# A hybrid attention layer on one core: the order's model learns VectorE's holds and TensorE's short waits, and two more pairs of heads add their halves on 128 rows

## The chip, the cores and the metric

The kernel runs on one core of a Trainium2 chip. The metric is the device time of one execution in microseconds. The engines are named as in the profile: PE is TensorE's matrix multiplication and PEld its weight loads, DVE is VectorE, ACT is ScalarE, POOL is GpSimd, SP is SyncE, which here issues transfers.

## The reference

One layer for 512 tokens of width 1024. A normalised input is multiplied by one wide matrix; its columns feed two token mixers and two gates. Branch a is latent attention with 8 heads (a low-rank query and key/value, a shared rotary key), branch b is 8 heads over the 128 keys that a small indexer picks for each query, with a bias by relative position. Both are causal by chunks of 64.

```python
h = rmsnorm(x, norm_g[l])
(q_lat, c_kv, k_rope, z_a, q_b, k_b, v_b, z_b, q_idx, k_idx, w_idx, gate_a, gate_b) = \
    jnp.split(h @ w_in[l], cuts, axis=-1)
...
y_a = mla_attention(q_nope, q_pe, k_nope, k_pe, v_a, pos) * jax.nn.silu(z_a)
y_b = dsa_attention(q_b, k_b, v_b, q_idx, k_idx, w_idx, rel_bias, pos, topk) * jax.nn.silu(z_b)
merged = (jax.nn.sigmoid(gate_a) * (y_a @ w_o_a[l])
          + jax.nn.sigmoid(gate_b) * (y_b @ w_o_b[l]))
x = x + merged @ w_out[l]
return rmsnorm(x, final_g)
```

## The kernel before, in words

Every operand of a product is split into a rounded high part (a cast on ACT, L382) and a low part, the rest (a subtraction on DVE or POOL, `lo_part`, L417 and L419). A product is three matmuls: high by high, high by low, low by high (`mm3`, L497). Many of the projections go in pairs, and the final product in blocks, by seven half-size products in place of eight (`seven`, `output`), whose sums DVE and POOL form.

The order of the work is not written out by hand. Each part of the kernel is a generator that yields steps, and a planner, `Flow`, runs them all at once while the program is made. It keeps a model of the time: for each engine when it is free, for each buffer when it was written and read last and by whom. For each waiting step it works out the earliest start, `start`, and takes the step with the least key: that start, plus 0.01 us for each unit of the thread's priority, and small handicaps for POOL and for changing the engine that holds the port that DVE and POOL share (`shares`). The instructions then stand on each engine in that order, and the engines wait for each other by semaphores. So a change to the model's numbers changes the order on all engines, and nothing in what is computed.

The steps that the change touches:

- `tt`, `stt` and `ts` make VectorE's two-input, three-input and one-input steps. `few` adds 0.12 us to a step on fewer than 128 rows.
- `with_values` multiplies the probabilities of one head by its values. The product of head h stands in a bank of PSUM on 64 rows of its own and 64 of its partner (the two halves are the high and the low part of the values). ACT copies the partner's rows to its own rows of a buffer `s_tmp`, and DVE adds 64 rows from the bank and 64 from the buffer into `s_y`. For pairs of heads in `YBOTH` both halves are copied by ACT, and when both heads of the pair are done one step adds 128 rows from SBUF, on DVE or POOL. Before, these are pairs 0, 1 and 2 of branch b.
- `rest` in `seven` makes the last four of the seven products, with priority `PREST`.
- `multiplier` works through a queue of projections, `jobs`, with priority 12. Behind the entries of `QUEUE` come the 16 projections of the branches' outputs (`branch_out`); the jobs that load and split `w_out` are put behind those numbered in `OUT_AT`, and the rest come last. `fetcher` issues the loads of the same queue on SP, as far as there are buffers (`NRAW`, `ROCAP`).
- `SPARE`, `TCAP` and `PCAP` set how many buffers a class of steps must leave free or may hold.

The phases in time: the first loads and the input's latents (to 46 us), projections beside the indexer's scores and branch a's heads (to some 180 us), the values of branch b (to 217), branch b's heads beside projections in pairs (to 331), the branches' output projections (to 377), the final product and norm.

Of the kernel before, what the change touches and what calls it, by code (L numbers as in the profile page):

```python
# [78 lines left out]
class View:  # L79
# [11 lines left out]
        return View(self.buf, self.ap.rearrange(pattern, **kw))  # L91

    @property
    def n(self):
        n = 1
        for s in self.ap.shape[1:]:
            n *= s
        return n


class Step:
# [5 lines left out]
    pair = False  # L107
    pbias = None
    rush = 0.0

    def __init__(self, options, outs, ins):
        self.options, self.outs, self.ins = options, outs, ins


class Get:
# [39 lines left out]
class Flow:  # L155
# [9 lines left out]
    def __init__(self, order):  # L165
        self.free = {"PE": 0.6, "ACT": 0.73, "DVE": 0.93, "POOL": 0.73, "SP": 0.73}
        self.hw, self.dma = 0.73, 0.0
        self.pbias = PEARLY
        self.port, self.holder, self.paired, self.pair = 0.0, None, 0.0, None
        self.order = order  # L170
        self.threads = []

    def spawn(self, gen, prio):
        t = Thread(gen, prio)
# [12 lines left out]
    def start(self, step, eng):  # L187
        s = 0.0
        for b in step.ins:
            if not b.written and b not in step.outs:  # L190
                return math.inf
            s = max(s, b.w + (RAW_LAG.get(eng, 0.0) if b.by == eng else self.lat(b.by, eng)))
            if b.bank and eng != "PE":
                for e, r in b.reads.items():
                    if e != eng:
                        s = max(s, r + self.lat(e, eng))
        for b in step.outs:
            if not eng == b.by == "SP":
                s = max(s, b.w + self.lat(b.by, eng))
            for e, r in b.reads.items():  # L200
                s = max(s, r + self.lat(e, eng))
        self.due = max(self.free[eng], s + SETTLE.get(eng, 0.0))
        s = max(s, self.free[eng])
        if self.shares(step, eng):
            s = max(s, self.port)
            if FENCE and eng == "POOL":
                if s < self.paired + FENCE:
                    s = max(s, self.paired + 0.17)
        return s

    @staticmethod
    def shares(step, eng):
# [2 lines left out]
    def run(self, stop=None):  # L215
        while self.threads:
            if stop and stop():
                return
            moved = False
            for t in sorted(self.threads, key=lambda t: t.prio):  # L220
                if isinstance(t.req, Get):
                    b = t.req.pool.give(t.req)
                    if b is not None:
                        self.advance(t, b)
                        moved = True
                elif isinstance(t.req, Until) and t.req.cond():
                    self.advance(t, None)
                    moved = True
            if moved:
                continue  # L230
            best = None
            for t in self.threads:
                if isinstance(t.req, Step):
                    for i, (eng, dur, emit) in enumerate(t.req.options):
                        s = self.start(t.req, eng)
                        change = SWITCH * (self.shares(t.req, eng) and eng != self.holder and s < self.port + 0.01)
                        key = (max(s, self.due) + change + BIAS * t.prio + t.off + YIELD * self.shares(t.req, eng) * (eng == "POOL") - t.req.rush, t.prio)
                        if len(t.req.options) > 1:
                            fin = s + dur + {"POOL": self.pbias if t.req.pbias is None else t.req.pbias, "ACT": t.req.abias}.get(eng, 0.0)
                            cand = (fin, s, eng, dur, emit, key)  # L240
                        else:
                            cand = (0.0, s, eng, dur, emit, key)
                        if i == 0 or cand[0] < mine[0]:
                            mine = cand
                    if best is None or mine[5] < best[1][5]:
                        best = (t, mine)
            if best is None or best[1][1] == math.inf:
                raise RuntimeError("stuck: " + "; ".join(f"{t.gen.__name__}@{t.gen.gi_frame.f_lineno} {type(t.req).__name__} {getattr(t.req, 'cls', '')}" for t in self.threads))
            t, (_, s, eng, dur, emit, _) = best
            step = t.req  # L250
            step.made = emit()
            step.fenced = s < self.paired + FENCE
            if eng == "SP":

                self.free["SP"] = s + 0.05
                kind = 0 if step.ins and step.outs else 1 if step.outs else 2
                if s > 25.0:
                    at = max(self.hw, s)
                    self.hw = at + 0.59
                    self.dma = max(self.dma, at + 1.0) + dur * SLOWER[kind]  # L260
                    end = self.dma + LAND[kind] + step.late
                else:
                    self.hw = max(self.hw, s) + (0.475 if kind else 0.65)
                    self.dma = max(self.dma, self.hw + 0.65) + dur
                    end = self.dma + (1.5 if s < 0.77 or dur < 0.05 else 2.15 if s < 10.0 else 1.8 if s < 20.0 else 1.0) + step.late
            else:
                self.free[eng] = end = s + dur
                if self.shares(step, eng):
                    self.port, self.holder = end, eng
                    if eng == "DVE":  # L270
                        self.paired, self.pair = end, step.made
                    elif step.fenced and self.pair:
                        self.order(step.made, self.pair)
                if step.moves:
                    self.dma = max(self.dma, end + (1.0 if eng == "POOL" else 0.8)) + step.moves
                    end = self.dma + (1.5 if s < 0.77 or step.moves < 0.05 else 2.0 if s < 3.0 else 1.0) + step.late
            for b in step.ins:
                b.r = b.reads[eng] = max(b.r, end)
                if isinstance(b, Part):
                    b.whole.r = b.whole.reads[eng] = max(b.whole.r, end)  # L280
            for b in step.outs:
                b.w = max(b.w, end)
                b.written, b.by = True, eng
                if isinstance(b, Part):
                    b.whole.w, b.whole.written, b.whole.by = max(b.whole.w, end), True, eng
            self.advance(t, None)
# [3 lines left out]
PEARLY = -0.5  # L290
BIAS = 0.01
SETTLE = {}
YIELD = 0.15
SWITCH = 0.1
JITTER = 0
SEED = 1
DRAWN = random.Random(SEED)
TC_ARGS = {}

# [2 lines left out]
def tile_block(ctx: ExitStack, tc: tile.TileContext, a: dict, out: bass.AP, bias_dram: bass.AP):  # L302
# [70 lines left out]
    def few(x):  # L373
        return 0.12 if x.ap.shape[0] < P else 0
# [38 lines left out]
    def tt(dst, x, y, op, engs=("DVE",)):  # L413
        opts = []
        for e in engs:
            if e == "DVE":
                opts.append(("DVE", 0.07 + 0.00104 * x.n + few(x), lambda: nc.vector.tensor_tensor(dst.ap, x.ap, y.ap, op=op)))  # L417
            else:
                opts.append(("POOL", 0.15 + 0.0021 * x.n, lambda: nc.gpsimd.tensor_tensor(dst.ap, x.ap, y.ap, op=op)))  # L419
        step = Step(opts, bufs(dst), bufs(x, y))  # L420
        step.pair = not (in_ps(x) or in_ps(y))
        return step

# [3 lines left out]
    def stt(dst, x, s, y, op0, op1):  # L427
        step = Step([("DVE", (0.13 if isinstance(s, View) else 0.07) + 0.00104 * x.n,
                      lambda: nc.vector.scalar_tensor_tensor(dst.ap, x.ap, sc(s), y.ap, op0=op0, op1=op1))],  # L429
                    bufs(dst), bufs(x, s, y))  # L430
        step.pair = not (in_ps(x) or in_ps(y))
        return step

    def ts(dst, x, s1, s2, op0, op1=None):
        t = 0.1 + (0.00104 if in_ps(x) else 0.00052) * x.n + few(x) + 0.03 * isinstance(s1, View)
        kw = {} if op1 is None else {"op1": op1}
        step = Step([("DVE", t, lambda: nc.vector.tensor_scalar(dst.ap, x.ap, sc(s1), s2, op0, **kw))],
                    bufs(dst), bufs(x, s1))
        step.pair = not in_ps(x) and x.n > 8
        return step  # L440

# [2059 lines left out]
QPOOL = 1  # L2501
PHCAP = 7
WCAP = 10
TCAP = 5
PTOPK = 17.0
PSCORE = 8.0
PFILL = 12.0
PHEAD = 8.0
OUT_AT = (0, 1, 2, 4, 6, 8, 10)
ORDER = [0,1,2,3]  # L2510
QUEUE = 'ga0 ga1 pe ma0 ga2 za0 va1 va0 ma1 ga3 za1 ma2 ga4 ga5 ma3 za2 za3 sb0 VB GA6 GA7 SB1 GB0 GB1 SB2 ZB0 ZB1 GB2 GB3 SB3 GB4 GB5 ZB2 ZB3 gb6 ou ou gb7 ou'
LATE = 0.75
# [2 lines left out]
ADDW = ()  # L2515
ADDP = ()
ADDV = ()
RUSH = 0.2
YBOTH = ((), (0, 1, 2))
BADD = 0  # L2520
AHEAD = 0
FENCE = 3.0
# [9 lines left out]
KEPT = 0  # L2532
LAND = 1.5, 1.3, 1.4
SLOWER = 1.8, 1.13, 1.09
TO_PE = 0.19
KMOVED = 1
APIECE = 0
PSEARCH = 10.0
PLOW = 9.0
PREST = 11.0  # L2540
SPARE = {'w': 3, 'wo': 6, 'sig': 3}
XOUT = 0
PSUMS = 5.0
PCAP = 12
BIAS_AT = ('a', 1)
NHELD = 3
ROCAP = 3
SUMS_AT = ('a', 4)
AWAY = (0, 1, 2, 3, 4, 5, 6, 7)

# [81 lines left out]
```

## Time and profile before

| | |
|---|---|
| median of 3 runs | 423.16 us (422.98 to 423.27) |
| the profiled execution | 422.26 us |
| its span | 420.5 us |
| mean granted TensorE clock | 0.997 |
| POOL busy | 92.2 us, 22% |
| bytes moved by DMA | 65.93 MB |

The span is the time from the first to the last instruction of the profiled execution; the execution's own time holds 1.76 us more. Busy time is the union of an engine's records. A matmul's record overlaps the next one's, so the pace of TensorE is read from the starts of neighbouring rows rather than from their durations. VectorE's records overlap as well, by some 0.08 us, where nothing holds the next one.

### The profile page before, as it was taken

Reading aid. Unit: us, or ns where it says so; the run is one execution under the profiler, and the core shown is the slowest. Engines: PE = TensorE matmul, PEld = TensorE weight load, DVE = VectorE, ACT = ScalarE, POOL = GpSimd, SP = SyncE. Lnnn points to the kernel's source line nnn. Section 1 sums busy time; section 2 is a strip of 40 time slices with the busy share of each in tenths; the row PEclk is TensorE's granted clock in tenths of the full one; section 3 lists DMA queues with packets and bytes.
Section 4 is the critical chain, followed back from the end, with each engine's and each line's share of the span. In section 5 each row is a group of like instructions: output and inputs, shape, how many; then the busy total and the mean of one; then the engine's idle time right before and its main releaser. Section 6 shows DMA issues by size and latency. Waiting matters only on the chain.

```text
span 420.5 us, 7598 instructions
## 1 busy us (share of the span) xinstructions
PE 412.1 (98%) x2523; PEld 369.8 (88%) x2523; DVE 382.9 (91%) x823; ACT 298.3 (71%) x684; POOL 92.2 (22%) x122
## 2 busy tenths in 40 slices
PE   8999999999999999999999999999999999999993
PEld 5999887898788888899999999999998888888883
DVE  4869799899999999999999988998889988999984
ACT  5785987575475757764768999999899854238533
POOL 1023777316562751410001110001000000020001
PEclk9999999999999999999999999999999999999998
DMA  8973356425435351334357418331843995465105
GB/s 258 396 282 118 89 181 182 146 78 127 153 91 162 124 165 50 76 90 151 101 200 186 139 43 213 134 109 45 228 136 119 342 383 175 150 213 188 51 2 200
DMA packets 30280, 65.93 MB, mean 157 GB/s; under 512 B 4648, under 2 KB 5688, under 8 KB 30240
## 3 DMA queue, kind: packets, MB, share of 16 engines
q1 hardware_dynamic: 29120, 63.82, 48.0%
q0 software_dynamic: 832, 1.22, 1.1%
q8 instruction: 20, 0.33, 0.3%
q10 hardware_dynamic: 288, 0.39, 0.3%
q14 instruction: 20, 0.16, 0.1%
HBM read 50.49 MB, written 4.21 MB: 130 GB/s over the span
## 4 chain that ended last, share of the span: by engine, by line
PE 78%; DVE 12%; DMA 3%; ACT 2%; issue 2%; SPq 1%; POOL 0%; POOLq 0%; DVEq 0%; ACTq 0%
PE ps L497 69%; PE ps L516 5%; DVE s_w L417 2%; DMA raw<-w_out 2%; DVE s_wo L417 1%; DVE mask L1002 1%; PE ps L976 1%; DVE s_rg L417 1%; PE ps L1932 1%; PE ps L1933 1%; PE ps L1934 1%; DVE raw L417 1%; DMA s_er<-w_kvl 1%; DVE s_xr L429 1%; DVE s_wsum L417 1%
## 5 line engine op out<-in xcount | busy, mean ns | idle before, releaser
L497 PE MATMUL ps<-s_h,s_w 128*128 128x512 f32 (+1 forms) x660 | 136.5, 343 | 0.4 <-ACT s_pair L382 0.4
L497 PEld LDWEIGHTS ps<-s_h,s_w 128*128 128x128 f32 x660 | 103.3, 190 | 11.6 <-ACT s_pair L382 0.6
L382 ACT CAST s_w<-raw 128x512 fp32r<-128x512 f32 (+2 forms) x118 | 68.3, 595 | 11.1 <-DVE raw L417 9.5
L417 DVE TENSOR_TENSOR s_w<-raw,s_w 128x512 fp32r<-128x512 f32 (+3 forms) x91 | 58.4, 659 | 2.7 <-ACT s_w L382 2.3
L497 PE MATMUL ps<-s_hs,s_w 128*128 128x256 f32 x432 | 59.1, 285 | 0.0
L497 PEld LDWEIGHTS ps<-s_hs,s_w 128*128 128x128 f32 x432 | 54.6, 191 | 0.2
L497 PE MATMUL ps<-s_ys,s_w 128*128 128x512 f32 x192 | 44.2, 390 | 0.0
L497 PEld LDWEIGHTS ps<-s_ys,s_w 128*128 128x128 f32 x192 | 35.9, 188 | 7.4
L419 POOL TENSOR_TENSOR s_w<-raw,s_w 128x512 fp32r<-128x512 f32 (+2 forms) x27 | 31.8, 1181 | 32.3 <-ACT s_w L382 12.7
L497 PE MATMUL ps<-s_w,s_xg 128*128 128x328 f32 (+1 forms) x192 | 33.1, 325 | 0.3
L497 PE MATMUL ps<-s_wo,s_mg 128*128 128x512 f32 (+1 forms) x156 | 33.0, 373 | 0.0
L497 PEld LDWEIGHTS ps<-s_w,s_xg 128*128 128x128 f32 x192 | 31.3, 188 | 1.2 <-ACT s_rbc L382 0.5
L497 PEld LDWEIGHTS ps<-s_wo,s_mg 128*128 128x128 f32 x156 | 27.6, 188 | 5.2
L391 ACT ACTIVATE s_p<-ps,sm 128x128 f32<-128x128 f32 (+3 forms) x32 | 16.9, 529 | 16.7 <-DVE sm L1916 16.6
L391 ACT ACTIVATE s_p<-s_p,sm 128x512 f32<-128x512 f32 (+3 forms) x48 | 26.8, 569 | 1.6 <-DVE sm L1879 1.4
L1001 DVE MAX8 sm<-mask 128x8 f32<-128x256 f32 (+2 forms) x48 | 25.8, 550 | 0.3 <-POOL mask L571 0.2
L1002 DVE MATCH_REPLACE8 mask<-sm,mask 128x256 f32<-128x256 f32 (+2 forms) x48 | 26.0, 544 | 0.0
L419 POOL TENSOR_TENSOR raw<-raw 128x512 f32<-128x512 f32 x4 | 5.2, 1296 | 93.8 <-DVE s_w L417 77.4
L516 PE MATMUL ps<-ident,s_p 128*128 128x128 f32 x160 | 23.3, 274 | 0.0
L382 ACT COPY s_pair<-ps 128x256 f32<-128x256 f32 (+1 forms) x40 | 15.7, 391 | 7.0 <-PE ps L497 6.8
L516 PEld LDWEIGHTS ps<-ident,s_p 128*128 128x128 f32 x160 | 18.4, 140 | 2.4 <-DVE s_ph L417 0.4
L497 PE MATMUL ps<-s_lat,s_w 128*128 128x512 f32 x78 | 19.9, 394 | 0.0
(222 smaller groups left out, 834.4 us busy)
## 6 DMA issues: line engine op xcount, KB each, us to landing
raw<-w_out SPq DMA_DIRECT2D x18, 512.0 KB, 5.9
s_op<-s_op SPq DMA_DIRECT2D x36, 128.0 KB, 2.6
raw<-w_ga SPq DMA_DIRECT2D x8, 512.0 KB, 3.7
raw<-w_gb SPq DMA_DIRECT2D x8, 512.0 KB, 4.1
s_ro<-w_o SPq DMA_DIRECT2D x16, 256.0 KB, 4.3
s_x<-xT SPq DMA_DIRECT2D x8, 256.0 KB, 5.0
s_xn<-x SPq DMA_DIRECT2D x8, 256.0 KB, 6.3
raw<-w_za SPq DMA_DIRECT2D x4, 512.0 KB, 4.5
```

What stands on the lines that cost most here:

```text
L382: nc.scalar.copy(dst.ap, src.ap)
L391: nc.scalar.activation(dst.ap, src.ap, func, **kw)
L417: opts.append(("DVE", 0.07 + 0.00104 * x.n + few(x), lambda: nc.vector.tensor_tensor(dst.ap, x.ap, y.ap, op=op)))
L419: opts.append(("POOL", 0.15 + 0.0021 * x.n, lambda: nc.gpsimd.tensor_tensor(dst.ap, x.ap, y.ap, op=op)))
L429: lambda: nc.vector.scalar_tensor_tensor(dst.ap, x.ap, sc(s), y.ap, op0=op0, op1=op1))],
L497: nc.tensor.matmul(ps.ap, l.ap, r.ap, start=start and i == 0, stop=stop and i == len(pairs) - 1, skip_group_check=more)
L516: nc.tensor.transpose(d.ap, s.ap, ident.tile)
L976: yield pe(0.005 + n / 2400, [ps.all], [qs[h].all, ks[0].all], lambda: (product_to(ps[:, :n], True), nc.tensor.matmul(ps.tile[:, :n], qs[h ...
L1001: yield Step([("DVE", t, lambda: nc.vector.max(m8.tile, work.ap))], [m8], [mask[i]])
L1002: yield Step([("DVE", t - 0.009, lambda: nc.vector.match_replace(work.ap, m8.tile, work.ap, MARK))], [mask[i]], [m8])
L1932: nc.tensor.matmul(o, q0[0:100], k0[0:100], start=True, stop=False)
L1933: nc.tensor.matmul(o, q0[0:96], k1[0:96], start=False, stop=False)
```

## The change

The planner's model is given three things. A VectorE step is charged 0.115 us when an input or the output starts at another group of 32 partitions than the last one in the same memory (`held`, `moved`, `on`, `place`); `few` is gone from `tt` and `ts`. A VectorE step that overwrites what VectorE itself read last is charged 0.115 us after that read (`REREAD`). A TensorE step is charged up to 0.1 us when an operand from another engine, or the reader of its bank, comes later than 0.1 us before TensorE is free (`LEAD`, `STALL`). Then a number of the planner's weights, caps and positions are other ones, and pairs 0 and 1 of branch a join `YBOTH`.

```diff
+    @property
+    def place(self):
+        whole = self.buf.tile
+        return self.buf.bank, (self.ap.offset - whole.offset) // (whole.ap[0][0] * 32)
...
             for e, r in b.reads.items():
-                s = max(s, r + self.lat(e, eng))
+                s = max(s, r + (REREAD.get(eng, 0.0) if e == eng else self.lat(e, eng)))
         self.due = max(self.free[eng], s + SETTLE.get(eng, 0.0))
+        if eng == "PE":
+            others = max([b.w + self.lat(b.by, eng) for b in (*step.ins, *step.outs) if b.by != eng] +
+                         [r + self.lat(e, eng) for b in step.outs for e, r in b.reads.items() if e != eng], default=0.0)
+            s = max(s, self.free[eng]) + min(STALL, max(0.0, others - self.free[eng] + LEAD))
+            return s
         s = max(s, self.free[eng])
+        if eng == "DVE" and self.held(step):
+            s = max(s, self.free[eng] + HELD)
...
+    def held(self, step):
+
+        out, ins = step.places()
+        return any(self.read.get(m, q) != q for m, q in ins) or out is not None and self.write.get(out[0], out[1]) != out[1]
+
+    def moved(self, step):
+        out, ins = step.places()
+        for m, q in reversed(ins):
+            self.read[m] = q
+        if out is not None:
+            self.write[out[0]] = out[1]
...
-YIELD = 0.15
+REREAD = {"DVE": 0.115}
+HELD = 0.115
+LEAD = 0.1
+STALL = 0.1
+YIELD = 0.05
...
-SEED = 1
+SEED = 37
...
-                opts.append(("DVE", 0.07 + 0.00104 * x.n + few(x), lambda: nc.vector.tensor_tensor(dst.ap, x.ap, y.ap, op=op)))
+                opts.append(("DVE", 0.07 + 0.00104 * x.n, lambda: nc.vector.tensor_tensor(dst.ap, x.ap, y.ap, op=op)))
...
-TCAP = 5
+TCAP = 7
...
-OUT_AT = (0, 1, 2, 4, 6, 8, 10)
+OUT_AT = (2, 3, 5, 9, 10, 11, 13)
...
-RUSH = 0.2
-YBOTH = ((), (0, 1, 2))
+RUSH = 0.0
+YBOTH = ((0, 1), (0, 1, 2))
...
-TO_PE = 0.19
+TO_PE = 0.27
...
-PREST = 11.0
-SPARE = {'w': 3, 'wo': 6, 'sig': 3}
+PREST = 8.0
+SPARE = {'w': 4, 'wo': 10, 'sig': 4}
...
-PCAP = 12
+PCAP = 14
...
-ROCAP = 3
+ROCAP = 4
```

`SEED` is used only through `JITTER`, which is 0 before and after. `YIELD` is POOL's handicap in the key, `RUSH` what is taken off the key of the power steps, `TO_PE` the model's latency from another engine to TensorE.

More of the change, by code (lines that the diff above doesn't have):

```diff
@@ L109, with on, places @@
     rush = 0.0
+    at = None
     def __init__(self, options, outs, ins):
         self.options, self.outs, self.ins = options, outs, ins
+    def on(self, out, *ins):
+        self.at = out.place, [v.place for v in ins]
+        return self
+    def places(self):
+        if self.at:
+            return self.at
+        return (self.outs[0].bank, 0) if self.outs else None, [(b.bank, 0) for b in self.ins]
 class Get:
@@ L171, in __init__ @@
         self.threads = []
+        self.read, self.write = {}, {}
     def spawn(self, gen, prio):
@@ L267, in run @@
                 self.free[eng] = end = s + dur
+                if eng == "DVE":
+                    self.moved(step)
                 if self.shares(step, eng):
@@ L416, in tt @@
             if e == "DVE":
-                opts.append(("DVE", 0.07 + 0.00104 * x.n + few(x), lambda: nc.vector.tensor_tensor(dst.ap, x.ap, y.ap, op=op)))
+                opts.append(("DVE", 0.07 + 0.00104 * x.n, lambda: nc.vector.tensor_tensor(dst.ap, x.ap, y.ap, op=op)))
             else:
                 opts.append(("POOL", 0.15 + 0.0021 * x.n, lambda: nc.gpsimd.tensor_tensor(dst.ap, x.ap, y.ap, op=op)))
-        step = Step(opts, bufs(dst), bufs(x, y))
+        step = Step(opts, bufs(dst), bufs(x, y)).on(dst, x, y)
         step.pair = not (in_ps(x) or in_ps(y))
@@ L429, in stt @@
                       lambda: nc.vector.scalar_tensor_tensor(dst.ap, x.ap, sc(s), y.ap, op0=op0, op1=op1))],
-                    bufs(dst), bufs(x, s, y))
+                    bufs(dst), bufs(x, s, y)).on(dst, x, y)
         step.pair = not (in_ps(x) or in_ps(y))
@@ L434, in ts @@
     def ts(dst, x, s1, s2, op0, op1=None):
-        t = 0.1 + (0.00104 if in_ps(x) else 0.00052) * x.n + few(x) + 0.03 * isinstance(s1, View)
+        t = 0.1 + (0.00104 if in_ps(x) else 0.00052) * x.n + 0.03 * isinstance(s1, View)
         kw = {} if op1 is None else {"op1": op1}
         step = Step([("DVE", t, lambda: nc.vector.tensor_scalar(dst.ap, x.ap, sc(s1), s2, op0, **kw))],
-                    bufs(dst), bufs(x, s1))
+                    bufs(dst), bufs(x, s1)).on(dst, x)
         step.pair = not in_ps(x) and x.n > 8
```

## The prediction

> **What bounds the kernel now.** I read the page first, then the busy time of each engine by stage, then the timeline of TensorE (PE) inside the stages.
>
> ```profile
> span 420.5 us, 7598 instructions
> PE 412.1 (98%) x2523; PEld 369.8 (88%) x2523; DVE 382.9 (91%) x823; ACT 298.3 (71%) x684; POOL 92.2 (22%) x122
> PE 78%; DVE 12%; DMA 3%; ACT 2%; issue 2%; SPq 1%; POOL 0%; POOLq 0%; DVEq 0%; ACTq 0%
> ```
>
> TensorE is busy in 98% of the span and carries 78% of the chain that ended last; VectorE (DVE) is second with 91%. The change touches no matmul of the product work, so it can only win time in which TensorE did less than it could. That time doesn't show as idle, because a matmul's record overlaps the next one's. The stages (columns: stretch, its length, busy time and instructions of each engine, clock, DMA share, GB/s):
>
> ```profile
> 0.00:7.00 7.00, 5.83 (x18) 2.78 (x19) 2.23 (x7) 3.59 (x7) 1.90 (x8) 1.00 0.70 213
> 46.00:180.00 134.00, 133.69 (x714) 112.95 (x712) 128.28 (x304) 93.45 (x221) 69.14 (x89) 1.00 0.43 125
> 217.00:331.00 114.00, 113.59 (x861) 109.01 (x860) 104.75 (x240) 106.52 (x263) 6.49 (x5) 1.00 0.50 145
> 331.00:377.00 46.00, 46.00 (x208) 38.24 (x207) 43.20 (x74) 19.52 (x36) 2.78 (x3) 1.00 0.71 246
> 377.00:414.20 37.20, 37.17 (x187) 31.44 (x185) 33.69 (x67) 21.34 (x47) 2.29 (x4) 1.00 0.30 106
> 414.20:420.50 6.30, 0.00 (x0) 0.00 (x0) 1.77 (x6) 2.06 (x3) 0.71 (x2) 0.78 0.45 168
> ```
>
> The first 7 us (first loads) and the last 6.3 us (last eviction, norm, store) hold almost no matmul. Between them I need TensorE's pace without a wait, from starts of neighbouring rows:
>
> ```profile
> 334.77 2.21 PE L497 MATMUL ps<-s_ys,s_w 128*128 128x512 f32 x9
> 336.82 0.97 PE L497 MATMUL ps<-s_ph,vv 128*128 128x512 f32 x4
> ...
> 250.73 3.04 PE L497 MATMUL ps<-s_hs,s_w 128*128 128x256 f32 x24
> 253.61 0.40 PE L497 MATMUL ps<-s_h,s_w 128*128 128x256 f32 x2
> ...
> 98.71 0.95 PE L516 MATMUL ps<-ident,s_p 128*128 128x128 f32 x7
> 99.41 2.32 PE L497 MATMUL ps<-s_h,s_w 128*128 128x512 f32 x9
> ```
>
> Nine matmuls of 512 columns pass in 336.82 - 334.77 = 2.05 us, 0.228 us each; 24 of 256 in 2.88 us, 0.120 each; seven of 128 in 0.70 us, 0.100 each. The groups of matmuls by shape, first and last row of 28 in 46 to 180 us, and of 14 in 217 to 331 us:
>
> ```profile
> L497 PE MATMUL ps<-s_h,s_w 128*128 128x512 f32 x288 | 76.3, 399 | 0.0
> ...
> L497 PE MATMUL ps<-s_w,s_xg 128*128 128x384 f32 x1 | 0.3, 341 | 0.0
> ...
> L497 PE MATMUL ps<-s_hs,s_w 128*128 128x256 f32 x348 | 48.1, 285 | 0.0
> ...
> L621 PE MATMUL ps<-zero 128*128 128x512 bf16 x1 | 0.4, 390 | 0.0
> ```
>
> In the first stretch the 28 rows add up to 412 matmuls of 512 columns, 47 of 384, two of 320, 111 of 256 and 142 of 128. With 0.175 for 384 and 0.145 for 320 (estimates, on the line between 0.120 and 0.228) that is 93.9 + 8.2 + 0.3 + 13.3 + 14.2 = 129.9 us. The stretch took 134.0, so about 4.1 us were lost. In the second, 82 of 512 (the filling of zeros among them), 30 of 384, 642 of 256 and 107 of 128 make 18.7 + 5.3 + 77.0 + 10.7 = 111.7 of 114.0: about 2.3 lost. Likewise 331 to 377 us, 199 of 512 columns and nine smaller, needs some 46 of 46.0: nothing lost. So **about 6.4 us of waits in TensorE's stream are all there is to win** between head and tail. They look like this:
>
> ```profile
> 112.99 0.44 PE L1932 MATMUL ps<-s_op,qhi 100*128 100x384 f32 x1
> 113.27 0.34 PE L1933 MATMUL ps<-s_op,qhi 96*128 96x384 f32 x1
> 113.44 0.34 PE L1934 MATMUL ps<-s_op,s_op 96*128 96x384 f32 x1
> ...
> 114.82 0.84 PE L497 MATMUL ps<-s_lat,s_w 128*128 128x512 f32 x3
> 115.95 0.50 PE L1932 MATMUL ps<-s_op,qhi 100*128 100x512 f32 x1 [0.28 <-ACT s_p L391]
> ...
> 216.77 0.88 PE L497 MATMUL ps<-s_h,s_w 128*128 128x256 f32 x6
> 218.06 1.70 PE L497 MATMUL ps<-s_h,s_w 128*128 128x256 f32 x12 [0.41 <-ACT s_pair L382]
> ```
>
> The first matmul of the step at 112.99 holds the stream 0.28 us where its twin at 113.27 takes 0.17: 0.11 us, and no idle time shows. Real starvation is rare: at 115.95 (1.13 us for 3 x 0.228, 0.45 lost) and at 218.06 (1.29 for 6 x 0.120, 0.57 lost). The two long ones make 1.0 us; the other 5.4 us are some fifty short waits of 0.11.
>
> **The change part by part.** (1) *TensorE's start in the planner* now costs up to 0.1 us where an operand from another engine comes later than 0.1 us ahead of the engine's free time, and operands count as 0.27 us on the way instead of 0.19. The planner then prefers another step that is long ready, if one stands within 0.1 of its key (0.01 per priority step). In both stretches there is filling work, the 288 and the 264 + 348 matmuls of projections, but it runs through one queue in a fixed order, and heads must advance. From below: no wait goes, 0. From above: all 5.4. I take 2.5, a little under half, since the short waits fall on the heads' own steps as often as on the filling that would have to replace them. The Trainium skill (TensorE: Matmul & The Clock Gate, on the reorder window) says that weight loads are pulled ahead of running matmuls; by that, a step whose operands come early enough shows no wait at all, and the sum would be -5.4.
>
> (2) *VectorE's holds.* The planner charges 0.115 us for a changed first partition and for a tile that is read just ahead of being overwritten.
>
> ```profile
> 131.44 0.67 DVE L1001 MAX8 sm<-mask 128x8 f32<-128x512 f32 x1
> 132.14 0.69 DVE L417 TENSOR_TENSOR s_y<-ps,s_tmp 64x512 f32<-64x512 f32 x1
> 132.87 0.29 DVE L1916 TENSOR_REDUCE sm<-ps 128x1 f32<-128x128 f32 x1
> ...
> 203.42 0.68 DVE L417 TENSOR_TENSOR s_wsum<-raw 128x512 f32<-128x512 f32 x1
> 204.14 0.69 DVE L417 TENSOR_TENSOR raw<-raw,raw 128x512 f32<-128x512 f32 x1
> 204.75 1.29 DVE L417 TENSOR_TENSOR vv<-s_pair,vv 128x512 fp32r<-128x512 f32 x2
> ```
>
> A 512-element step hands over after 0.61 us (204.14 to 204.75); around the add on 64 rows it is 0.70 and 0.73, and ahead of the overwritten `raw` 0.72: 0.1 each, so the charge fits. It removes work from no path by itself; what it may save in order is inside the 2.5.
>
> (3) *Output halves.* Four heads of branch a now do what three pairs of branch b do:
>
> ```profile
> L417 DVE TENSOR_TENSOR s_y<-ps,s_tmp x10: 664/686/697, 100.0 to 338.9; 64x512 f32<-64x512 f32 x10
> L382 ACT COPY s_y<-ps x6: 565/582/601, 241.8 to 302.3; 64x512 f32<-64x512 f32 x6
> L417 DVE TENSOR_TENSOR s_y<-s_y,s_tmp x3: 679/681/685, 250.6 to 304.7; 128x512 f32<-128x512 f32 x3
> L419 POOL TENSOR_TENSOR s_y<-s_y,s_z x1: 1310/1310/1310, 107.3 to 107.3; 128x512 f32<-128x512 f32 x1
> ```
>
> Four adds of 0.686 us leave VectorE and two of 0.681 come (or none, if POOL takes them at 1.31): -1.4 to -2.7 us, with two odd heads' holds (4 x 0.11) about -1.8 to -3.2. ScalarE (ACT) gets four copies of 0.582, +2.3 us. These lie in 46 to 180 us, where VectorE has 128.28 of 134.0 and ScalarE 93.45: ScalarE has 40 us of room, and the price is nothing on the path unless a copy stands ahead of a probability's exponential, then 0.58 once or twice. VectorE's gain isn't on the path either, but makes operands come earlier. I count 0. The Trainium skill (SBUF — State Buffer, who interferes with whom) speaks against it: an add with two SBUF inputs contends with a GpSimd instruction that reads SBUF and may wait for all of it, where an add from PSUM doesn't. No row here shows such a collision of the pair; by that rule two adds would wait up to 1.31 us each, and VectorE's gain would be gone, the span unchanged.
>
> (4) *Moved weights and caps.* Seven of the 18 `w_out` jobs stand two to five branch projections later in the queue (first ones behind job 2, 3 and 5 instead of 0, 1 and 2). Each such job is a load of 512 KB on the SP queue, two casts and two subtractions:
>
> ```profile
> L417 DVE TENSOR_TENSOR s_wo<-raw,s_wo 128x512 fp32r<-128x512 f32 x12 | 7.9, 684 | 0.0
> ```
>
> that is 2 x 0.684 = 1.37 us of VectorE per job, beside the casts. On SP the `w_o` loads, which stood behind them, come earlier. VectorE has 46.0 - 43.20 = 2.8 us free in 331 to 377 and 37.2 - 33.69 = 3.5 in 377 to 414: room for two jobs, so I count 0. The larger caps (TCAP, PCAP, ROCAP) and SPARE only allow or keep back buffers, 0. The last four products of each set of seven get priority 8 instead of 11; both stand ahead of the filling (12), 0. The dropped haste of the power steps and POOL's smaller handicap change who adds, not how much, 0. Head and tail keep their chains: 0. A filling of zeros more or less is 0.23 us.
>
> **Sum.** The profiled execution took 422.26 us, 1.76 around its span of 420.5. The sum is -2.5: span 418.0, execution 419.8. The median of the runs, 423.16, lies 0.9 above the profiled one; so 420.7 for the median.
>
> **The rivals.** *Nothing gained*: a greedy order that avoids a late operand here meets one elsewhere; heads and projections both hang on the same VectorE at 95%. For it: the short waits are spread evenly, 4.1 us in 134 and 2.3 in 114. Against it: the present order was made without any price on them. Time 422.3 to 424.0. *All short waits go*, and perhaps the one at 218: -5.4 and, with the 0.57, -6.0: 417.2 to 417.8 (the skill's rule of the reorder window, as above). For it: most are 0.11, the price now charged. *Slower*: the later `w_out` jobs pile up on VectorE behind 377 us. It decides from the third job on that slides across: three make 33.69 + 4.1 = 37.8 against 37.2, +0.6; five make 40.5, +3.3, less what part (1) keeps. Time 424.0 to 426.5. For it: VectorE's 91% there; TensorE has no other work left. Against: all seven stay ahead of the last two branch projections. That the change doesn't do what it says is hardly a rival: the order is made from it.
>
> **How the numbers follow.** Forecast, some of the short waits gone (418.5 to 422.3): 0.47. All gone (below 418.5): 0.13. Nothing (422.3 to 424.0): 0.17. Slower (above 424.0): 0.23. A measurement of this kernel tells 0.2% (0.85 us) from no change. Faster: 0.47 + 0.13, less a little at 422.3: 0.60; the same 0.17; slower 0.23. The range leaves out about a tenth at each end: 417.4 to 425.4.
>
> **What would show it.** Right: the same count of matmuls of each shape; TensorE's loss in 46 to 180 and 217 to 331 us down from 6.4 to about 4; six adds `s_y<-ps,s_tmp`, ten copies `s_y<-ps`, five adds on 128 rows; 331 to 414 us as dense as now; a tail of 6.3 us. Wrong: idle marks of a microsecond before matmuls of `s_wo`, a longer head, or short waits as many as before.

## The result, and the profile after

The changed kernel takes 419.81 us, median of 6 runs (419.51 to 420.35), beside 422.65 (421.93 to 423.27) for the kernel before, also a median of 6 (three of them are the runs listed under the time before): a ratio of 0.9935, 95% interval 0.9925 to 0.9946. That is 2.84 us less; 2.5 were forecast. The profiled execution took 419.51 us with a span of 417.7.

The page of the kernel after (busy time by engine, then the chain that ended last, by engine):

```profile
span 417.7 us, 7583 instructions
PE 409.7 (98%) x2523; PEld 369.3 (88%) x2523; DVE 380.4 (91%) x822; ACT 302.3 (72%) x694; POOL 86.5 (21%) x115
PE 90%; issue 6%; POOL 1%; DVE 1%; ACT 0%; POOLq 0%; DVEq 0%; ACTq 0%
```

The shares say next to nothing: 98% and 91% as before. TensorE has the same 2523 matmuls. The chain now runs through TensorE for 90% instead of 78%, and through VectorE for 1% instead of 12%. The same stretches of time as before:

```profile
46.00:180.00 134.00, 134.00 (x722) 114.50 (x721) 127.71 (x302) 97.35 (x231) 65.36 (x81) 1.00 0.44 128
217.00:331.00 114.00, 114.00 (x858) 109.43 (x857) 103.48 (x236) 104.03 (x254) 4.17 (x4) 1.00 0.54 164
331.00:377.00 46.00, 46.00 (x215) 38.34 (x214) 42.99 (x78) 21.93 (x42) 3.23 (x4) 1.00 0.57 198
377.00:414.20 37.20, 34.48 (x175) 29.24 (x173) 34.23 (x69) 22.06 (x48) 2.23 (x4) 1.00 0.29 104
```

The columns are those of the prediction's table. More matmuls pass in 46 to 180 us (722 for 714), and the last stretch ends early. With the prediction's own paces, the shapes in 46 to 180 us now need 131.3 of 134.0 us and those in 217 to 331 us 113.6 of 114.0: 3.1 us lost, where it was 6.4. The stages up to 377 us stay dense, and the tail behind the last matmul is 6.2 us (6.3 before).

The outputs of the heads, by the instructions on tile `s_y` (count, then least, median and greatest duration in ns):

```profile
L424 ACT COPY s_y<-ps x10: 571/582/587, 100.9 to 307.5; 64x512 f32<-64x512 f32 x10
L459 DVE TENSOR_TENSOR s_y<-ps,s_tmp x6: 673/688/695, 151.6 to 342.3; 64x512 f32<-64x512 f32 x6
L459 DVE TENSOR_TENSOR s_y<-s_y,s_tmp x4: 675/682/686, 106.7 to 309.0; 128x512 f32<-128x512 f32 x4
L461 POOL TENSOR_TENSOR s_y<-s_y,s_tmp x1: 1294/1294/1294, 129.6 to 129.6; 128x512 f32<-128x512 f32 x1
```

The pairs' edit is as read from the diff: ten copies, six adds on 64 rows, five on 128. VectorE's holds can be seen directly. In the timeline of VectorE after:

```profile
151.03 0.68 DVE L1044 MATCH_REPLACE8 mask<-sm,mask 128x512 f32<-128x512 f32 x1
151.63 0.67 DVE L459 TENSOR_TENSOR s_y<-ps,s_tmp 64x512 f32<-64x512 f32 x1
152.23 0.54 DVE L459 TENSOR_TENSOR s_ph<-ps,s_ph 128x384 fp32r<-128x384 f32 x1
...
184.39 0.68 DVE L459 TENSOR_TENSOR s_w<-s_wsum,s_w 128x512 fp32r<-128x512 f32 x1
184.99 0.68 DVE L459 TENSOR_TENSOR raw<-raw,raw 128x512 f32<-128x512 f32 x1
185.59 0.68 DVE L459 TENSOR_TENSOR s_w<-s_wsum,s_w 128x512 fp32r<-128x512 f32 x1
```

The 64-row add stands 0.60 us behind its neighbour, and so does the step that overwrites `raw`, for another step now lies between it and the last reader. I count a hold where a VectorE step starts 0.02 to 0.06 us after the end of the record before it, instead of 0.08 before that end: 62 in the kernel before, 31 after.

**What the losses of TensorE are.** For each matmul I took the time to the next one's start, less 0.015 us + columns / 2400 (the pace of the wide rows in the prediction; for 128 columns, which I call narrow, less 0.109 us, their usual distance), from 6.9 us on, and kept losses over 0.04 us. They fall into three kinds. The first is a surprise. In the timeline of TensorE after:

```profile
101.70 0.49 PE L558 MATMUL ps<-ident,s_p 128*128 128x128 f32 x3
101.95 1.63 PE L539 MATMUL ps<-s_h,s_w 128*128 128x512 f32 x6
103.42 0.80 PE L539 MATMUL ps<-s_ph,vv 128*128 128x512 f32 x3
...
106.08 0.23 PE L1974 MATMUL ps<-s_op,qhi 100*128 100x128 f32 x1
106.14 0.27 PE L1975 MATMUL ps<-s_op,qhi 96*128 96x128 f32 x1
106.25 0.28 PE L1976 MATMUL ps<-s_op,s_op 96*128 96x128 f32 x1
106.36 0.33 PE L1974 MATMUL ps<-s_op,qhi 100*128 100x256 f32 x1
106.53 0.28 PE L1975 MATMUL ps<-s_op,qhi 96*128 96x256 f32 x1
106.65 0.28 PE L1976 MATMUL ps<-s_op,s_op 96*128 96x256 f32 x1
106.77 1.53 PE L539 MATMUL ps<-s_h,s_w 128*128 128x512 f32 x6
108.14 0.41 PE L1974 MATMUL ps<-s_op,qhi 100*128 100x384 f32 x1
108.40 0.34 PE L1975 MATMUL ps<-s_op,qhi 96*128 96x384 f32 x1
108.57 0.34 PE L1976 MATMUL ps<-s_op,s_op 96*128 96x384 f32 x1
```

Six matmuls of 512 columns take 103.42 - 101.95 = 1.47 us behind three of 128 columns, and 108.14 - 106.77 = 1.37 behind some of 256. The 0.1 us is lost at the first wide matmul behind narrow ones, also where no instruction there waits for a semaphore. This is no wait; I call it the *return*. Its sizes repeat: 0.085 us for 512 columns behind transposes, 0.080 for 256, 0.046 behind the two narrow matmuls of a head's values.

The return isn't lost at the turn, though, for the narrow matmuls ahead of it are short by as much. Neighbours of 128 columns stand 0.11 us apart (106.14 to 106.25 and to 106.36). But of the three transposes at 101.70, which take 0.25 us, the last hands over after 0.03, and the first of the three at 106.08 takes 0.06. Those three and the 256 columns behind them take 106.53 - 106.08 = 0.45 us: 0.12 for 256 columns, as ever, and three times 0.11. In the kernel before, over the 25 places where nothing waits, two narrow matmuls with the turn behind them add 0.217 us (median), three 0.332, four 0.439 and five 0.526: 0.105 to 0.111 for each, and nothing is left for the turn. So the returns below are a part of the price of the narrow matmuls. The count of these is the same in every order, and a return by itself is nothing to win.

The second kind is the *short wait*, under 0.25 us, at a matmul that waits or follows one that did: at 108.14 (0.26 for 0.17). A loss of 0.18 us that stands at 233 us in both kernels isn't counted. The third is the *starvation* over 0.25 us. In us:

| | returns | short waits | starvation |
|---|---|---|---|
| before | 67: 4.81 | 26: 2.45 | 3: 1.32 |
| after | 64: 4.61 | 13: 1.03 | 2: 0.89 |

Waits and starvation went from 3.77 to 1.92 us, -1.85, and the tail -0.10; TensorE's first 6.9 us, where the warming-up matmuls run, lost 0.54 less. That is 2.5 of the 2.8 us of span. The 0.54 doesn't come from the change: in the first 15 us every engine has the same instructions in the same order in both kernels. An early cast on ACT (`s_w<-s_er`) starts at 5.71 us before and at 5.10 after, so the two executions differ there by themselves. The 21st matmul starts at 7.32 us before and at 6.78 after, and over all fourteen kernels at 6.77 to 7.59; the 6.77 belongs to a kernel that gained next to nothing (VectorE's charges off, retuned).

### The profile page after: what moved, and what is told of

Its sections match the earlier page's. It is cut to its first block, busy times and chain, and to the rows that moved or that the text cites. A ratio compares the mean times of both kernels' runs of the same rounds, so it can differ in the third digit from the quotient of the medians.

```text
span 417.7 us, 7583 instructions
## 1 busy us (share of the span) xinstructions
PE 409.7 (98%) x2523; PEld 369.3 (88%) x2523; DVE 380.4 (91%) x822; ACT 302.3 (72%) x694; POOL 86.5 (21%) x115
## 4 chain that ended last, share of the span: by engine, by line
PE 90%; issue 6%; POOL 1%; DVE 1%; ACT 0%; POOLq 0%; DVEq 0%; ACTq 0%
PE ps L539 80%; PE ps L558 5%; PE ps L1975 1%; PE ps L1974 1%; PE ps L1976 1%; PE ps L1018 1%; ACT junk L433 0%; POOL rstd L511 0%; POOL sm L511 0%; DVE s_rg L459 0%; POOL ident L572 0%; DVE s_xr L459 0%; POOLq L2670 0%; ACT s_rbc L424 0%; POOL glat L572 0%
## 5 line engine op out<-in xcount | busy, mean ns | idle before, releaser
L539 PE MATMUL ps<-s_h,s_w 128*128 128x512 f32 (+1 forms) x660 | 131.8, 342 | 0.0
L424 ACT CAST s_w<-raw 128x512 fp32r<-128x512 f32 (+2 forms) x118 | 67.2, 593 | 4.1 <-DVE raw L459 2.7
L459 DVE TENSOR_TENSOR s_w<-raw,s_w 128x512 fp32r<-128x512 f32 (+2 forms) x91 | 58.0, 656 | 3.9 <-ACT s_w L424 3.8
L539 PE MATMUL ps<-s_hs,s_w 128*128 128x256 f32 x432 | 60.5, 285 | 0.0
L539 PE MATMUL ps<-s_ys,s_w 128*128 128x512 f32 x192 | 45.4, 392 | 0.0
L433 ACT ACTIVATE s_p<-s_p,sm 128x256 f32<-128x256 f32 (+3 forms) x55 | 30.3, 565 | 2.0 <-DVE sm L2057 1.6
L459 DVE TENSOR_TENSOR s_ph<-ps,s_ph 128x512 fp32r<-128x512 f32 (+1 forms) x32 | 18.7, 612 | 0.9 <-ACT s_ph L424 0.9
```

The costliest lines, as they stand in the source:

```text
L424: nc.scalar.copy(dst.ap, src.ap)
L433: nc.scalar.activation(dst.ap, src.ap, func, **kw)
L459: opts.append(("DVE", 0.07 + 0.00104 * x.n, lambda: nc.vector.tensor_tensor(dst.ap, x.ap, y.ap, op=op)))
L539: nc.tensor.matmul(ps.ap, l.ap, r.ap, start=start and i == 0, stop=stop and i == len(pairs) - 1, skip_group_check=more)
```

## The experiments

The theory at first was the prediction's part (1): TensorE's charge for late operands makes the waits fewer. The rivals: the other weights did it, VectorE's charges did it, or the order is a lucky one. All ratios are to the kernel before, run on the same chip. The counts by the definitions above, outside the stretches of a reduced clock:

| kernel | ratio | holds | returns | short waits | starvation |
|---|---|---|---|---|---|
| TensorE's charge off | 1.0198 | 45 | 60: 4.42 | 17: 1.60 | 9: 7.09 |
| VectorE's charges off | 1.0008 | 54 | 65: 4.80 | 25: 2.71 | 4: 3.13 |
| new model, old weights and pairs | 1.0183 | 41 | 68: 4.78 | 23: 1.95 | 7: 8.19 |
| old model, new weights and pairs | 1.0005 | 50 | 63: 4.41 | 23: 1.92 | 5: 1.98 |
| after, shuffled, 1 | 1.0164 | 44 | 67: 4.79 | 15: 1.24 | 5: 8.43 |
| after, shuffled, 2 | 1.0204 | 41 | 65: 4.62 | 15: 1.59 | 8: 8.37 |
| before, shuffled, 1 | 1.0211 | 43 | 65: 4.72 | 34: 3.83 | 9: 7.28 |
| before, shuffled, 2 | 1.0020 | 51 | 67: 4.87 | 31: 3.09 | 6: 2.44 |
| before, new pairs alone | 1.0020 | 61 | 64: 4.61 | 30: 3.01 | 4: 1.80 |
| TensorE's charge off, retuned | 0.9928 | 42 | 65: 4.58 | 9: 0.78 | 1: 0.31 |
| VectorE's charges off, retuned | 0.9988 | 56 | 62: 4.46 | 25: 2.46 | 5: 1.59 |
| after, retuned | 0.9915 | 31 | 62: 4.44 | 14: 1.35 | 1: 0.31 |

**First round: one part undone, or one alone.** The expectations count returns and short waits together, since the two weren't told apart yet: in the first two rounds as losses of 0.07 to 0.14 us (59 before, 46 after), in the third of 0.06 to 0.25 us (64 before, 53 after).

```diff
-STALL = 0.1
+STALL = 0.0
```

> The changed kernel with STALL = 0, so the planner no longer charges TensorE's steps for late operands; all else as changed. Theory (the gain is the short waits that this charge avoids): the short waits of 0.07 to 0.14 us in TensorE's stream, 59 before and 46 after, go back to 55 to 62, and the time to about 0.998 of the kernel before. Rival (the other weights and caps made the gain): waits stay near 46 and the ratio stays at 0.993 to 0.995.

1.0198 (1.0178 to 1.0217), 431.6 us. Neither ratio held. The count falls to 42, nearer to the rival's 46 than to the theory's 55 to 62, and the time goes up by 8.8 us: TensorE starves at 323 to 334 us. The waits of TensorE in this kernel (us in total, times, longest):

```profile
PE ps L558 <- DVE s_ph L459: 1.9, 2, 1.6
PE ps L558 <- ACT s_p L433: 1.6, 2, 1.3
PE ps L539 <- ACT s_ys L433: 1.1, 1, 1.1
```

```diff
-REREAD = {"DVE": 0.115}
-HELD = 0.115
+REREAD = {}
+HELD = 0.0
```

> The changed kernel with HELD = 0 and REREAD empty, so VectorE's holds cost nothing in the planner. Theory: holds on VectorE, 62 before and 31 after, go back to about 60, some 3.5 us more VectorE time that is not on TensorE's path: ratio 0.993 to 0.996. Rival (VectorE's holds are what delays operands): the ratio goes back to 0.998 or more, with more waits on TensorE.

1.0008 (0.9993 to 1.0023): the rival's number. Holds are back at 54, short waits at 25, and one wait of 1.8 us for POOL stands at 176 us. The twelve runs fall into two groups, five at 422.3 to 422.8 us and seven at 424.0 to 424.4; the profile with that wait is of the upper one. `few` isn't put back in this run; it stands in the fourth.

The third run takes the changed model with `YIELD`, `RUSH`, `TCAP`, `OUT_AT`, `YBOTH`, `TO_PE`, `PREST`, `SPARE`, `PCAP` and `ROCAP` of the kernel before; the fourth takes the model before with the new ones.

> The new model with all weights, caps, positions and the pairs of heads of the kernel before. Theory (the model's charges make the gain): ratio 0.994 to 0.996, waits near 46. Rival (the weights do): 0.999 to 1.001, waits near 59.

1.0183 (1.0160 to 1.0207). Neither number held: TensorE starves for 8.2 us, 6.1 of them at 170 to 180 us.

> The model of the kernel before with the new weights, caps, positions and pairs of heads. Theory: 0.998 to 1.002, short waits near 59. Rival (the weights make the gain): 0.993 to 0.996.

1.0005 (0.9992 to 1.0018), as the theory had it, but with a count of 44 where 59 had been expected. And whatever was undone, all of the gain was gone, and two kernels lost 8 us, more than any part can be worth. An order that is made step by step changes everywhere behind the first step that differs, so each of these runs compares two whole orders.

**Second round: how much an order varies by itself.**

```diff
-JITTER = 0
-SEED = 37
+JITTER = 0.02
+SEED = 1
```

> The changed kernel with a random number of up to 0.02 us added to each step's key (JITTER = 0.02, SEED = 1), a change that means nothing. Theory (the charges make the gain, whatever the order in detail): ratio 0.991 to 0.997, short waits 42 to 52. Rival (the gain hangs on this one order, and each run so far that undid a part lost it because it made another order): ratio above 0.998, with one or more starvations of TensorE over 0.5 us.

1.0164 (1.0125 to 1.0203). The output of this order is wrong, and so is that of the next (relative errors of 1.06 and 1.18), for a reason that isn't known. Both are taken as timings of an order, with that reserve; they are no kernels to use.

> The same with SEED = 2; the same numbers. Theory: both shuffles within 0.991 to 0.997. Rival: the two differ from each other by more than 0.4% and at least one lies above 0.998.

1.0204 (1.0184 to 1.0225). The rival is right for the time: both lie far above 0.998, though by only 0.4% from each other. Where the second one loses it, in the timeline of TensorE:

```profile
394.81 2.43 PE L539 MATMUL ps<-s_wo,s_mg 128*128 128x512 f32 x10
402.34 2.08 PE L539 MATMUL ps<-s_wo,s_mg 128*128 128x512 f32 x4 [5.10 <-DVE s_wo L459]
```

5.1 us of starvation in the final product, for a split of `w_out` on VectorE.

> The kernel before with JITTER = 0.02, SEED = 1. Theory: 0.998 to 1.004, since its model knows nothing of the charges. Rival (the order before was as lucky a draw as the one after): 1.004 to 1.025, with new starvations of TensorE.

1.0211 (1.0187 to 1.0235), the rival's number, with nine starvations.

> The kernel before with JITTER = 0.02, SEED = 2. Theory: 0.998 to 1.004, and close to the first shuffle. Rival: 1.004 to 1.025, and the two shuffles differ by more than 0.4%.

1.0020 (1.0010 to 1.0031). So the kernel before is a well-chosen order as well: one shuffle costs it 2.1%, the other 0.2%. The starvation column (2.4 to 8.4 us against 1.3 and 0.9) is what an unchosen order has. The short waits tell another story: 15 and 15 for the shuffles of the kernel after, like its own 13; 34 and 31 for those of the kernel before, like its 26. In these six kernels that property goes with the planner and not with one order.

**Third round: each model with an order chosen for it.** To compare models rather than accidents, `BIAS`, `RUSH` and a few other weights were moved in each until its own plan ended about as early as that of the kernel after.

```diff
-STALL = 0.1
+STALL = 0.0
-BIAS = 0.01
+BIAS = 0.009
-RUSH = 0.0
+RUSH = 0.2
```

> The changed kernel without TensorE's charge (STALL = 0), as in the run that starved, but with BIAS 0.009 in place of 0.01 and RUSH 0.2 in place of 0, chosen so that the planner's plan ends early again. Theory (the charge itself makes the short waits fewer): no starvation over 1 us, but short waits back at 60 or more, ratio 0.998 to 1.001. Rival (an order without starvation is all that counts, and the new caps thin out the waits): short waits 45 to 55, ratio 0.992 to 0.996.

0.9928 (0.9914 to 0.9942), 419.71 us: the whole gain without TensorE's charge, with a count of 45 and nine true short waits, the fewest of all. The theory falls, and the rival's numbers hold. Its waits of TensorE, as the profile shows them, come down to one, at the start:

```profile
PE ps L663 <- DVE neghalf L613: 1.0, 1, 1.0
```

```diff
-REREAD = {"DVE": 0.115}
-HELD = 0.115
+REREAD = {}
+HELD = 0.0
-YIELD = 0.05
+YIELD = 0.1
-RUSH = 0.0
+RUSH = 0.2
-TO_PE = 0.27
+TO_PE = 0.2
```

> The changed kernel without VectorE's charges (HELD = 0, REREAD empty), with YIELD 0.1, RUSH 0.2 and TO_PE 0.2, chosen so that the plan ends early again. Theory: holds near 55 again, but the ratio 0.992 to 0.996. Rival (late operands come from holds that the plan does not know): holds near 55, short waits 60 or more as in the first run without these charges, ratio 0.997 to 1.001.

0.9988 (0.9978 to 0.9997): without VectorE's charges an order chosen in the same way gains 0.5 us. Holds are 56 and short waits 25, as in the first run without these charges. The rival is right in the ratio and the holds; its count is 58, a little under the 60 that it had. Among its waits:

```profile
PE ps L1975 <- DMA s_op<-kpel: 0.2, 1, 0.2
PE ps L1974 <- ACT s_p L433: 0.2, 1, 0.2
PE ps L539 <- ACT s_pair L424: 0.2, 1, 0.2
```

These are late operands of the heads and pairs in small amounts; there is no single place.

```diff
-TO_PE = 0.27
+TO_PE = 0.25
-RUSH = 0.0
+RUSH = 0.1
```

> The changed kernel with all its charges, TO_PE 0.25 in place of 0.27 and RUSH 0.1 in place of 0, the earliest end that the full model gave. Theory (the charges fit the chip): ratio 0.990 to 0.9945, short waits 48 to 55, no starvation over 0.6 us: as fast as the changed kernel or up to 1 us faster. Rival (a plan's end says nothing below a microsecond): 0.995 or more.

0.9915 (0.9902 to 0.9927), 419.33 us, within the theory's range, with no starvation over 0.31 us. It is the fastest kernel here: below the changed one's 0.9935 (0.9925 to 0.9946), though the intervals touch. One thing that it mends can be named. The kernel after starves at its early norm:

```profile
PE ps L558 <- POOL rstd L511: 0.4, 1, 0.4
```

0.57 us are lost there by the starts of the matmuls, at 27.8 us. The three kernels of the first round with `RUSH` at 0 wait 0.3 to 0.6 us for the same step; all three retuned kernels, with `RUSH` at 0.1 or 0.2, don't, and neither did the kernel before at 0.2. So the change gave that half microsecond back. That `RUSH` did it isn't shown: the two shuffles of the kernel after, with `RUSH` at 0, don't wait there either.

**The pairs alone**, in the kernel before:

```diff
-YBOTH = ((), (0, 1, 2))
+YBOTH = ((0, 1), (0, 1, 2))
```

> The kernel before with nothing changed but YBOTH, so pairs 0 and 1 of branch a add on 128 rows. Theory (the pairs cost and give nothing on TensorE's path): ratio 0.998 to 1.002 unless the new order starves TensorE; VectorE's holds fall by 4 to 8, short waits stay near 64. Rival (the copies by ScalarE stand ahead of exponentials): 1.003 or more with waits for ScalarE before the heads' products.

1.0020 (1.0012 to 1.0029), 0.7 us slower. Holds stay at 61, where 4 to 8 fewer were expected. 0.5 us of it is more starvation, 0.6 more short waits, 0.2 fewer returns; that is the size of one shuffle, so a price of the pairs isn't shown, and a gain from them alone is ruled out in this order.

## Why the prediction was right, and where its reasons were wrong

*The size and the sign* were right: -2.84 us for -2.5. The size is luck in part. It is that of a chosen order: the two shuffles of the new kernel are 2.3 and 2.7% slower than it. In the profiles, some 0.5 us of the gain stands in the first 7 us, where the order of the work is the same in both kernels, and the budget was wrong. *The budget* was "about 6.4 us of waits in TensorE's stream are all there is to win", with "some fifty short waits of 0.11". There were 26 short waits, 2.45 us, and 1.32 us of starvation. About 2.2 us of the 6.4 is the price of the narrow matmuls: the 249 of them in the two stretches were priced at 0.100, from a row of seven whose last one hands over early, where each costs 0.109 once the return is counted in. What could be won by order was 3.8 us, of which the change took 1.85. So a little under half of too large a budget came out near the truth; of the 2.45 us of short waits, my "a little under half" would have given 1.1.

*Part (1)*, TensorE's charge, was named as the cause, and isn't shown to be one: without it a chosen order is as fast (0.9928), with as few short waits. The full model retuned, 0.9915, isn't shown to be faster than that, for the intervals overlap. *Part (2)*, VectorE's holds, was put at "removes work from no path by itself", and what it may save inside the 2.5 that part (1) earns. That step failed. In the six kernels with VectorE's charges and the new weights, short waits number 9 to 17 (mean 13.8, 1.27 us); in the seven without the charges, 23 to 34 (mean 27.7, 2.78 us). The two groups don't overlap, whatever the order, and they don't without the two shuffles whose output is wrong (9 to 17 over four kernels). The charges by themselves are not enough: with the old weights and pairs the count is 23. The retuned kernel without the charges moved only three weights, so a wider search without them, at the new weights, is a rival that wasn't tried. Which of the new weights is needed stays open, and so does the path from a hold to a late operand, which I haven't followed in a trace; that the plan's times come nearer to the chip's is argued, not shown.

*Part (3)*, the pairs, 0 on the path: the count of instructions was right, and alone they gave 1.0020. The collision with POOL that the prediction weighed doesn't show: the four adds on VectorE took 0.675 to 0.686 us, and no POOL record stands beside them. *Part (4)*, the moved weights, 0: with the pairs and without the charges they gave 1.0005, and the order after has no starvation in the last stage, as expected. *The rival that ends slower* had the right mechanism: a queue on VectorE behind 377 us that starves the final product happens in both shuffles of the kernel after, 5 us each. It didn't happen in the order that was chosen. *The rival of no gain*, that late operands turn up elsewhere, describes several of the orders above better than this one.

The Trainium skill's rule of the reorder window (TensorE: Matmul & The Clock Gate), as the prediction read it beside part (1), would have emptied TensorE's stream of 5.4 us. The runs show why that can't be had here: only 2.45 us of it were short waits.

## What to carry to other kernels

Before a gap is called a wait, look whether the instruction there waits for anything, and whether the gap repeats with the shape of its neighbours; a fixed price is no room for an order. Price a stretch of narrow matmuls together with the first wide one behind it. Where a planner makes the order, undoing one of its numbers compares two whole orders: shuffle it meaninglessly first to see the spread (here a shuffle cost 0.2 to 2.7% of its own kernel's time), count what the model is meant to change (waits, holds) over all of the orders, and give each variant an order chosen with the same care.

## What the runs showed of the hardware

A starvation costs more than its length, for the granted clock falls behind it. In the first shuffle of the kernel after, the stages around its 5 us of starvation (the clock is the third column from the end):

```profile
390.00:400.00 10.00, 10.00 (x45) 8.27 (x45) 9.69 (x19) 8.77 (x19) 0.00 (x0) 1.00 0.04 14
400.00:406.00 6.00, 1.13 (x8) 0.78 (x6) 6.00 (x12) 0.62 (x1) 1.27 (x1) 0.95 0.00 0
406.00:410.00 4.00, 3.88 (x13) 3.40 (x14) 1.27 (x3) 0.00 (x0) 0.00 (x0) 0.50 0.00 0
410.00:416.00 6.00, 6.00 (x29) 5.19 (x29) 2.72 (x6) 1.75 (x6) 0.00 (x0) 0.82 0.01 3
416.00:424.00 8.00, 8.00 (x48) 7.02 (x46) 4.96 (x13) 3.95 (x10) 1.31 (x3) 1.00 0.35 132
```

VectorE is full while TensorE stands, and TensorE then runs at 0.50 for 4 us and 0.82 for 6 more: by the clock's own records it is reduced for 6.8 us, some 3 us lost on top of 5. The same follows the starvations of the kernels with TensorE's charge off and with the old weights, and it is part of why the slow orders lie 2% off. No single long gap is needed. With TensorE's charge off the longest idle time at 323 to 334 us is 1.6 us, and the clock's records have 0.50 for 3.4 us twice, from 328.1 and from 334.9:

```profile
325.00:330.00 5.00, 3.10 (x13) 2.38 (x14) 4.06 (x11) 4.02 (x10) 0.00 (x0) 0.81 1.04 388
330.00:335.00 5.00, 3.35 (x17) 2.52 (x16) 2.84 (x5) 3.90 (x8) 0.00 (x0) 0.84 0.36 135
335.00:340.00 5.00, 5.00 (x21) 4.24 (x20) 3.96 (x9) 3.53 (x10) 0.00 (x0) 0.67 0.01 3
```

The Trainium skill (TensorE: Matmul & The Clock Gate, the HAM clock gate) says that the clock halves after an idle window of about 3.4 us and comes back after as long a busy one. The traces agree with the 0.50 and with the length: behind every starvation that lowers the clock it stays down for 3.4 or 6.8 us, one or two such windows. They don't agree that a window has to be idle throughout, as the 1.6 us show.

The price of the narrow matmuls was the other thing that I hadn't expected: 0.109 us each for 128 columns, where 0.015 us + columns / 2400 gives 0.068. Over the 260 of them in this kernel that is some 11 us. In a timeline it stands in two places, as a slow pace between narrow neighbours and as the return at the first wide matmul. Since two to five of them cost the same each, fewer turns wouldn't win it back; whether fewer narrow matmuls would wasn't tried.
